# A planned four-layer trunk: pricing each change of the TensorE array's shape by kind, with new unit durations, a fixed SBUF layout and a new table of priorities

## The chip, the cores and the metric

The kernel runs on one core of one Trainium2 chip. The metric is the device time in microseconds of one execution: the median of three runs. Beside them stands one profiled execution with its trace.

## What is computed

The reference is a trunk of four residual layers, x of shape (1, 256, 1024) in float32. Layer i takes token mixer i mod 3, and every layer is followed by a SwiGLU block:

```python
for i in range(DEPTH):                       # DEPTH 4
    kind, j = i % N_MIXERS, i // N_MIXERS    # N_MIXERS 3
    h = rms_norm(x, norm_mix[i])
    if kind == 0: ...                        # RWKV-7 time mixing
...
def swiglu(h, w_gu, w_down):                 # D_FF 2816
    g, u = jnp.split(h @ w_gu, 2, axis=-1)
    return (jax.nn.silu(g) * u) @ w_down
...
def step(state, inp):                        # in rwkv7_time_mix, 256 steps, 16 heads x 64
    r_t, w_t, k_t, v_t, kk_t, a_t = inp
    sa = jnp.einsum('bhvk,bhk->bhv', state, kk_t)
    state = (state * w_t[:, :, None, :]
             - sa[..., None] * (kk_t * a_t)[:, :, None, :]
             + v_t[..., None] * k_t[:, :, None, :])
    return state, jnp.einsum('bhvk,bhk->bhv', state, r_t)
```

Layer 0 and layer 3 are RWKV-7, layer 1 is stick-breaking attention (`log_sigmoid` of the scores with a reversed cumulative sum over earlier keys), layer 2 is sparse attention over the 64 keys that an indexer of 8 heads picks for each query. Each mixer has input projections of 1024 x 1024 and an output projection; RWKV also has low-rank ("lora") projections for its decay, gate and rates.

## The kernel before, in words

**Layout of the work.** The activations lie transposed in SBUF, features on the 128 partitions in 8 chunks (`NC`), 256 tokens along the free dimension. Weights come from HBM as pieces of 128 x 1024 float32 (`raw`, 4 slots). A piece is split in two fp32r parts: a cast makes the high part `wh` (on ScalarE or VectorE), a subtraction on VectorE makes the low part `wl`; activations are split in the same way (`kx`, `gx`, `prx`, `h`, `prhl` and others). A product of 128 output features, `gemm1`, then takes for each chunk one matmul of wh with both parts of x (512 columns) and one of wl with the high part (256 columns).

**Stages.** The four layers and their SwiGLU blocks follow each other. An RWKV layer (`rwkv`, L1092) has a head (token shift `pre`, mixed inputs `xm`, their split halves, the first projections), the lora products, the rates and decays, then for chunks of 64 tokens the blocks of a triangular system. Their 32 x 32 diagonal parts are inverted on VectorE in 31 dependent steps (a multiplication into `blocks`, an addition into `inv`) with a stream transpose ahead of it and behind it. Four copies or so then move the result into `XT`; `combine` makes one more stream transpose (`xd`) for each of four pairs of head chunks, and two groups of 32 x 32 matmuls (`cmb1`, `cmb2`) complete the inverse. The recurrence over four chunks (`Chain.step`) then runs as four chains of small matmuls: pS (state by PR), Y from PR, xu (XT by u0), qu (the state's update), Y from SB. Beside all this stand the gate `pg` (a product with weights) and the bonus term, in which VectorE multiplies a sum `bn` by `vf` into `pr`, with `prs` and its halves `prhl` as steps.

**What sets the order.** Nothing is emitted directly. The kernel's code calls `Queue` objects, and `record` (L347) keeps each instruction as an `Op` with a cost from `_cost` (L263). Several matmuls may be put into one op with `unit` (L325), which may be given a duration in ns in place of the sum of its parts. An operation called on `any` has alternatives on two engines, for instance a cast on ScalarE or VectorE. `schedule` (L723) runs sixteen rounds of list scheduling over five engines (`_schedule`, L471), each with ranks from the order of the round before (`_place`), and one more round after `_nudge` has added random offsets to ranks: each row of the table `NUDGES` is a seed, a range of operations and a width. The plan with the earliest planned end is kept. `emit` (L766) then takes the SBUF slots in order of first use, those of a size that is a multiple of 128 first, and writes the instructions in planned order; each engine works through its own in that order. All instructions recorded by the plan therefore carry one line of the program, L788.

**The array's shape.** In the trace a matmul's form stands as rows by columns of the array: 128*128, 64*64, 128*64, 32*32 and so on. The planner knows only a flag, `op.parts`: either side spans at most 64 partitions. When the flag differs from that of TensorE's last operation, `_schedule` adds `SWITCH` = 95 ns to the operation's cost, and `choose` holds the operation back for another one with the same flag, unless that one's rank lies more than `STICK` = 1000 below. Where TensorE would be idle for long, `keep_warm` puts in pairs of bf16 matmuls without use (`warm_o`, L1893).

Of the kernel before, what the change touches and what calls it, by code (L numbers as in the profile page):

```python
# [14 lines left out]
F32R = mybir.dt.float32r  # L15
# [45 lines left out]


# [118 lines left out]
class Op:  # L181


    def __init__(self, eng):
        self.eng, self.instrs, self.cost, self.table, self.cols = eng, [], 0.0, None, 0.0
        self.preds, self.succs, self.alts, self.warmer, self.parts = set(), [], {}, False, False
        self.end, self.bufs, self.ns, self.lag, self.lands = 0.0, [], 0.0, 0.0, False
        self.banks = []


class Queue:
# [63 lines left out]
SWITCH = 95.0  # L255

STICK = 1000.0
# [51 lines left out]
class Plan:  # L309
# [37 lines left out]
    def record(self, eng, method, args, kw):  # L347
# [19 lines left out]
        if eng == "tensor":  # L367
            op.cols += _columns(method, outs[0], ins)
            op.parts = outs[0].p1 - outs[0].p0 <= 64 or ins[0].p1 - ins[0].p0 <= 64
# [101 lines left out]
    def _schedule(self, counts, reserve):  # L471
        engines = ("tensor", "vector", "scalar", "gpsimd", "sync")
        ready, pending, free = ({e: v() for e in engines} for v in (list, list, float))
        out, recent, parts = [], collections.deque(), False
# [68 lines left out]
        def keep_warm(t, until):  # L543

            nonlocal parts, hot
# [14 lines left out]
            t, parts = t + (SWITCH if parts else 0.0), False  # L560
# [25 lines left out]
        def choose(e, t):  # L586
# [3 lines left out]
            while ready[e] and got is None:  # L590
# [17 lines left out]
                if watch and o.parts != parts and held is None and not o.alts:  # L608
# [3 lines left out]
                if held and (o.parts != parts or o.rank < held[0][2].rank - STICK):  # L612
# [20 lines left out]
        while done < len(self.ops):  # L633
# [39 lines left out]
            if e == "tensor":  # L673
                if filled(t) < 0.8 * BUSY:
                    cost *= 2
                if o.parts != parts:
                    parts, cost = o.parts, cost + SWITCH
# [88 lines left out]
    def emit(self, nc, counts, warmer):  # L766
# [12 lines left out]
        for k in sorted(first, key=lambda k: size[k] % 128 > 0):  # L779
            first[k].get()  # L780
# [11 lines left out]
def trunk(ctx: ExitStack, tc: tile.TileContext, xT_in, vecs_in, wts, lora_in, consts_in, id32_in, nqk_in, outT, order, layers=None):  # L792
# [299 lines left out]
    def rwkv(j, layer, after):  # L1092
# [119 lines left out]
        for p in range(0, NC, 2):  # L1212
            pw = bank("lw"), bank("la")
            with unit(2, 960.0):
# [106 lines left out]
        for p in range(NC):  # L1321
            o = bank("sc"), bank("sc")
            with unit(2):
# [734 lines left out]
```

## Time and profile before

| what | value |
|---|---|
| runs | 1368.5 us median of 3 (1368.15 to 1368.95) |
| profiled execution | 1368.04 us |
| its span, first to last instruction | 1366.2 us, 25568 instructions |
| mean granted clock of TensorE | 1.000 |
| ScalarE's largest group | 350 casts `wh<-raw`, 1050 ns each |
| VectorE's largest group | 383 subtractions `wl<-raw,wh`, 1221 ns each |
| TensorE's largest group | 704 matmuls `gate<-xg,wh`, 392 ns each |
| read from HBM | 217.36 MB, in 401 pieces of 512 KB and a few more |
| busy share of the DMA queue's engines | 50.2% |

The span is the time between the first and the last instruction; the profiled execution is 1.8 us longer. PE is TensorE, DVE is VectorE, ACT is ScalarE; PEld stands for weight loads, which run beside the matmuls. Durations of matmuls overlap, so the time that one takes is read from start to start. The busy shares of all engines are shown in the prediction.

### The profile page before, as it was taken

To read this page: it belongs to the slowest core of one execution; us is meant where nothing else is said; L and a number is where in the kernel's file an instruction comes from. 1 tells how busy PE (TensorE), PEld (TensorE's weight loads), DVE (VectorE), ACT (ScalarE), POOL (GpSimd) and SP (SyncE) were. 2 spreads that over 40 slices of the span, in tenths; PEclk is the share of its full clock that TensorE was granted. 3 is DMA by queue.
4 is the path that set the end of the run, shared out by engine and by line. 5 is a ranking of instruction groups with operands and counts; after the bars stand their busy time and mean duration, and the time that the engine had idled before them with its cause. 6 is when DMAs were issued, how large, how long until landed. Compare 5 with 4: busy or idle time off the path is not lost.

```text
span 1366.2 us, 25568 instructions
## 1 busy us (share of the span) xinstructions
PE 1357.6 (99%) x10202; PEld 1189.5 (87%) x10202; DVE 1124.7 (82%) x1954; ACT 796.0 (58%) x1342; POOL 12.2 (1%) x18
## 2 busy tenths in 40 slices
PE   9999999999999999999999999999999999999998
PEld 8988898888888898888887798888899888988887
DVE  8999689886677788886679998887599996888864
ACT  7966755454455765544455965554388366665542
POOL 0100000000000000000000000000000000000000
PEclk9999999999999999999999999999999999999999
DMA  6423156555655345655654445556544231656553
GB/s 243 149 84 119 44 175 198 187 187 180 193 175 153 126 151 186 191 194 196 210 183 139 163 137 187 185 187 198 185 123 130 77 108 51 184 184 188 187 190 116
DMA packets 61335, 220.07 MB, mean 161 GB/s; under 512 B 6816, under 2 KB 8352, under 8 KB 60960
## 3 DMA queue, kind: packets, MB, share of 16 engines
q1 hardware_dynamic: 61216, 218.44, 50.2%
q8 instruction: 80, 1.31, 0.4%
q14 instruction: 39, 0.32, 0.1%
HBM read 217.36 MB, written 1.05 MB: 160 GB/s over the span
## 4 chain that ended last, share of the span: by engine, by line
PE 92%; DVE 6%; DMA 1%; issue 1%; ACT 0%; SPq 0%; DVEq 0%; ACTq 0%
PE dn L788 18%; PE gate L788 18%; PE up L788 18%; PE po L788 7%; PE qk L788 3%; PE vps L788 3%; PE rp L788 3%; PE kp L788 2%; PE z L788 2%; PE vp L788 2%; PE q L788 2%; PE k L788 2%; PE Y L788 1%; DVE blocks L788 1%; PE sc L788 1%; PE attn_o L788 1%
## 5 line engine op out<-in xcount | busy, mean ns | idle before, releaser
L788 ACT CAST wh<-raw 128x1024 fp32r<-128x1024 f32 x350 | 366.3, 1050 | 343.7 <-PE dn L788 110.1
L788 DVE TENSOR_TENSOR wl<-raw,wh 128x1024 fp32r<-128x1024 f32 x383 | 461.6, 1221 | 76.8 <-ACT wh L788 69.6
L788 PE MATMUL gate<-xg,wh 128*128 128x512 f32 x704 | 263.4, 392 | 0.0
L788 PE MATMUL up<-xg,wh 128*128 128x512 f32 x704 | 262.7, 392 | 0.0
L788 PE MATMUL dn<-h,wh 128*128 128x512 f32 (+1 forms) x720 | 246.3, 389 | 0.0
L788 PE MATMUL dn<-h,wl 128*128 128x256 f32 x704 | 197.2, 280 | 0.0
L788 PE MATMUL gate<-xg,wl 128*128 128x256 f32 x704 | 197.1, 280 | 0.0
L788 PE MATMUL up<-xg,wl 128*128 128x256 f32 x704 | 197.1, 280 | 0.0
L788 PEld LDWEIGHTS dn<-h,wh 128*128 128x128 f32 x720 | 134.0, 188 | 30.0
L788 PEld LDWEIGHTS up<-xg,wh 128*128 128x128 f32 x704 | 131.7, 187 | 28.8
L788 PEld LDWEIGHTS gate<-xg,wh 128*128 128x128 f32 x704 | 131.7, 187 | 28.6
L788 PEld LDWEIGHTS gate<-xg,wl 128*128 128x128 f32 x704 | 133.0, 189 | 0.1
L788 PEld LDWEIGHTS up<-xg,wl 128*128 128x128 f32 x704 | 133.1, 189 | 0.1
L788 PEld LDWEIGHTS dn<-h,wl 128*128 128x128 f32 x704 | 132.8, 189 | 0.0
L788 ACT CAST h<-gus 128x512 fp32r<-128x512 f32 x43 | 26.7, 621 | 53.0 <-DVE gus L788 52.9
L788 PE MATMUL vp<-xv,raw 128*128 128x256 f32 x256 | 57.3, 382 | 0.3 <-PE qct L788 0.3
L788 DVE TENSOR_TENSOR gus<-gus,rstd 128x512 f32<-128x512 f32 x88 | 57.2, 684 | 0.2
L788 PEld LDWEIGHTS vp<-xv,raw 128*128 128x128 f32 x256 | 48.0, 190 | 7.7 <-issue 0.7
L788 DVE TENSOR_TENSOR h<-gus,h 128x512 fp32r<-128x512 f32 x44 | 30.4, 691 | 24.8 <-ACT h L788 24.8
L788 PE MATMUL rp<-prx,wh 128*128 128x256 f32 x256 | 49.7, 295 | 0.0
L788 PE MATMUL kp<-kx,wh 128*128 128x256 f32 x256 | 48.4, 288 | 0.5 <-DVE kx L788 0.4
L788 PE MATMUL po<-yhl,wh 128*128 128x256 f32 x256 | 48.3, 289 | 0.0
(331 smaller groups left out, 2432.2 us busy)
## 6 DMA issues: line engine op xcount, KB each, us to landing
raw<-in_wts_dram SPq DMA_DIRECT2D x401, 512.0 KB, 3.9
lora<-in_lora_dram SPq DMA_DIRECT2D x2, 1280.0 KB, 9.7
xt<-in_xT_dram SPq DMA_DIRECT2D x4, 256.0 KB, 4.0
lora<-in_lora_dram SPq DMA_DIRECT2D x2, 512.0 KB, 5.3
inv<-in_id_dram SPq DMA_DIRECT2D x2, 512.0 KB, 3.6
out_dram<-xt SPq DMA_DIRECT2D x8, 128.0 KB, 2.9
sbt<-in_consts_dram SPq DMA_DIRECT2D x1, 512.0 KB, 3.9
consts<-in_consts_dram SPq DMA_DIRECT2D x1, 288.0 KB, 5.8
```

Source lines behind the costliest of these rows:

```text
L788: getattr(getattr(nc, o.eng), method)(*map(real, args), **{k: real(a) for k, a in kw.items()})
```

## The change

It has four parts, all of them in the planner or in the numbers that it works with.

1. *The array's shape by kind.* `op.parts` gives way to `op.shape`, the shape of the operation's first and last matmul in quarters of the array (1, 2 or 4 by 1, 2 or 4), and `op.enter`, a price by the shape that is entered. A change costs `SWITCH` (now 97) and `enter`; `choose` holds back an operation of any other shape and not only one with another flag. The planner starts in the full shape `WHOLE`, and warming matmuls bring it back there.
2. *Unit durations* become smaller where the old ones held such a change, or are given for the first time.
3. *A fixed SBUF layout.* `emit` takes the slots in the order of a list of names, `LAYOUT`, within the two groups of sizes.
4. *A new table of priorities*, 56 rows in place of 63.

```diff
+LAYOUT = (
+    "ones xt0 chmask xt1 xt2 xt3 sqa_0 QC_0 sq_0 s0_0 raw_0 s1_0 t_0 s6_0 raw_1 raw_2 t_1 t_2 t_3 raw_3 wh_0 wl_0 wh_1 wh_2 "
...
-        self.preds, self.succs, self.alts, self.warmer, self.parts = set(), [], {}, False, False
+        self.preds, self.succs, self.alts, self.warmer, self.shape, self.enter = set(), [], {}, False, [], 0.0
...
 NUDGES = [[
-    (461406, 4825, 4945, 1000), (222252, 5820, 5870, 3000), (292571, 81, 131, 1000), (91922, 1777, 1897, 1000),
...
+    (886415, 620, 640, 8000), (374831, 1759, 2059, 1000), (804050, 3305, 3605, 300), (41355, 3292, 3592, 300),
...
-SWITCH = 95.0
+SWITCH = 97.0
+WHOLE = (4, 4)
+ENTER = {(2, 4): 100.0, (1, 4): 100.0, (4, 2): 48.0, (2, 2): 48.0, (1, 1): 18.0, (4, 1): 18.0}
...
-            op.parts = outs[0].p1 - outs[0].p0 <= 64 or ins[0].p1 - ins[0].p0 <= 64
+            shape = tuple(-(-(v.p1 - v.p0) // 32) for v in (ins[0], outs[0]))
+            shape = tuple(n if n < 3 else 4 for n in shape)
+            if not op.shape:
+                op.enter = ENTER.get(shape, 100.0 if ins[0].dtype == F32R else 0.0)
+            op.shape = [(op.shape or [shape])[0], shape]
...
-                if watch and o.parts != parts and held is None and not o.alts:
+                if watch and o.shape[0] != shape and held is None and not o.alts:
...
-                if held and (o.parts != parts or o.rank < held[0][2].rank - STICK):
+                if held and (o.shape[0] != shape or o.rank < held[0][2].rank - STICK):
...
-                if o.parts != parts:
-                    parts, cost = o.parts, cost + SWITCH
+                if o.shape[0] != shape:
+                    cost += SWITCH + o.enter
+                shape = o.shape[1]
...
-        for k in sorted(first, key=lambda k: size[k] % 128 > 0):
+        def place(k):
+            n = k if isinstance(k, str) else k.name
+            return size[k] % 128 > 0, LAYOUT.index(n) if n in LAYOUT else len(LAYOUT)
+
+        for k in sorted(first, key=place):
             first[k].get()
```

The unit durations in ns, before and now: lw and la 960 to 860; sc from the sum of its parts to 900; qct 560 to 460; vtok 990 to 934; bv 980 to 934; cmb1 and cmb2 540 to 512; pS, Y, xu and qu 280 to 232; pv from the sum of its parts to 628; z of the stick-breaking layer 1000 to 976; idx 740 to 655; z of the sparse layer 1000 to 1098.

What is computed, and the matmuls that do it, stay the same; the order on each engine and the choice of the engine for operations with alternatives come out anew. Three places show it.

TensorE, in the recurrence of the first RWKV layer, behind the fourth group of 32 x 32 matmuls in the order before (pS, Y<-PR and xu are of the form 64*64, qu and Y<-SB of the form 128*64; x4 counts the matmuls of one group):

```order
L788 MATMUL cmb1_1824<-xd_1671,SB_1088 32x32 x16
L788 MATMUL pS_1845<-Sn_1814,PR_824 64x64 x4
L788 MATMUL Y_1852<-SB_1018,UV_1275 64x64 x4
L788 MATMUL qu_1859<-UV_1275,QC_857 64x64 x4
L788 MATMUL xu_1865<-u0_1857,XT_913 64x64 x4
L788 MATMUL Y_1764<-SB_1018,UV_1275 64x64 x4
L788 MATMUL Y_1852<-PR_824,Sn_1814 64x64 x4
```

and the same stretch in the new order (where the line of recorded instructions is L803):

```order
L803 MATMUL cmb1_1728<-xd_1636,SB_1087 32x32 x16
L803 MATMUL qu_1748<-UV_1355,QC_715 64x64 x4
L803 MATMUL qu_1754<-UV_1355,QC_715 64x64 x4
L803 MATMUL Y_1761<-SB_1022,UV_1355 64x64 x4
L803 MATMUL Y_1767<-SB_1022,UV_1355 64x64 x4
L803 MATMUL pS_1779<-Sn_1759,PR_821 64x64 x4
L803 MATMUL Y_1761<-PR_821,Sn_1759 64x64 x4
L803 MATMUL pS_1795<-Sn_1772,PR_821 64x64 x4
L803 MATMUL xu_1802<-u0_1793,XT_914 64x64 x4
L803 MATMUL Y_1767<-PR_821,Sn_1772 64x64 x4
```

Before, the six groups behind cmb1 take up a shape five times; now two groups of qu and two of Y<-SB stand together, then five groups of 64*64, and the nine take up a shape twice.

VectorE, at the end of the first RWKV layer's inverse, up to the transpose xd that opens `combine`, before (prhl is the split of the bonus term, vf are the layer's values):

```order
L788 TENSOR_TENSOR inv_1001<-inv_1001,blocks_1083 128x2x30
L788 CAST prhl_1476<-prs_1449 128x512
L788 TENSOR_TENSOR blocks_1083<-inv_1001 128x31
L788 TENSOR_TENSOR pr_1133<-bn_1416,vf1_114 128x512
L788 TENSOR_TENSOR inv_1001<-inv_1001,blocks_1083 128x31
L788 TENSOR_TENSOR prhl_1500<-prs_1449,prhl_1476 128x512
L788 STREAM_TRANSPOSE blocks_1083<-inv_1001 128x1024
L788 TENSOR_TENSOR pr_1133<-bn_1421,vf0_113 128x512
L788 COPY XT_913<-blocks_1083 32x16x32 x3
L788 COPY XT_925<-blocks_1083 32x16x32
L788 STREAM_TRANSPOSE xd_1569<-XT_913 128x512
```

and now:

```order
L803 TENSOR_TENSOR inv_981<-inv_981,blocks_1074 128x2x30
L803 TENSOR_TENSOR wl24_1447<-raw24_1258,wh24_1334 128x1024
L803 TENSOR_TENSOR blocks_1074<-inv_981 128x31
L803 TENSOR_TENSOR inv_981<-inv_981,blocks_1074 128x31
L803 STREAM_TRANSPOSE blocks_1074<-inv_981 128x1024
L803 COPY XT_914<-blocks_1074 32x16x32 x4
L803 CAST prhl_1531<-prs_1467 128x512
L803 STREAM_TRANSPOSE xd_1537<-XT_914 128x512
L803 TENSOR_TENSOR prhl_1558<-prs_1467,prhl_1531 128x512
L803 TENSOR_TENSOR pr_1133<-bn_1513,vf2_116 128x512
```

Of the two products with vf between the last steps of the inverse and xd, one has gone ahead and one behind (vf1, which is further down the new order); one subtraction of prhl has gone behind xd, and a wl has come among the last steps. The four copies of XT now stand together.

VectorE, at the same place of the last RWKV layer, before:

```order
L788 TENSOR_TENSOR blocks_11400<-inv_11297 128x31
L788 TENSOR_TENSOR wl325_11826<-raw325_11633,wh325_11658 128x1024
L788 TENSOR_TENSOR inv_11297<-inv_11297,blocks_11400 128x31
L788 TENSOR_TENSOR wy_11643<-raw326_11620,wy_11643 32x1024
L788 STREAM_TRANSPOSE blocks_11400<-inv_11297 128x1024
L788 TENSOR_TENSOR pr_11469<-bn_11847,vf0_113 128x512
L788 COPY XT_11242<-blocks_11400 32x16x32 x3
L788 TENSOR_TENSOR prhl_11930<-prs_11894,prhl_11920 128x512
L788 TENSOR_TENSOR pr_11469<-bn_11898,vf1_114 128x512
L788 STREAM_TRANSPOSE xd_11941<-XT_11242 128x512
L788 STREAM_TRANSPOSE xd_11951<-XT_11242 128x512
```

and now:

```order
L803 TENSOR_TENSOR pr_11388<-bn_11825,vf0_113 128x512
L803 TENSOR_TENSOR inv_11301<-inv_11301,blocks_11424 128x31
L803 COPY QC_11240<-bv_11839 128x8x64
L803 STREAM_TRANSPOSE blocks_11424<-inv_11301 128x1024
L803 TENSOR_TENSOR prhl_11911<-prs_11837,prhl_11880 128x512
L803 COPY XT_11252<-blocks_11424 32x16x32
L803 TENSOR_SCALAR prs_11909<-pr_11388,vecs_127 128x256
L803 COPY XT_11252<-blocks_11424 32x16x32 x2
L803 COPY QC_11240<-bv_11892 128x8x64
L803 STREAM_TRANSPOSE xd_11947<-XT_11252 128x512
L803 TENSOR_TENSOR prhl_11957<-prs_11909,prhl_11939 128x512
L803 TENSOR_TENSOR pr_11388<-bn_11834,vf1_114 128x512
```

Two copies from bv into QC, which ScalarE made before, stand among VectorE's rows ahead of the first xd; of the two products with vf ahead of it one has gone behind.

At the head of the first layer, VectorE's subtraction wl of the second weight piece moves from behind the first of the kx splits to behind the second. Some operations with alternatives change sides: of eight casts into prx VectorE keeps one and not four, of sixteen scalings into am it takes eight and not four, of eight copies from bv into QC two and not none, and ScalarE takes the rest of each.

More of the change, by code (lines that the diff above doesn't have):

```diff
@@ L60 @@
 CSPLIT = [0, COFF["ntri"][0], COFF["dupi"][0], NCONST]
+LAYOUT = (
+    "ones xt0 chmask xt1 xt2 xt3 sqa_0 QC_0 sq_0 s0_0 raw_0 s1_0 t_0 s6_0 raw_1 raw_2 t_1 t_2 t_3 raw_3 wh_0 wl_0 wh_1 wh_2 "
+    "wh_3 t2_0 xm_0 t2_1 xm_1 PR_0 xm_2 consts0 wl_1 xm_3 identb bonesr t2_2 wl_2 t_4 t2_3 wl_3 s7_0 xb_0 SZ_0 t2_4 dc_0 vf0 "
+    "vf1 vf3 vf2 t_5 t_6 t_7 kc0_0 kc1_0 kc2_0 eps_rms SA_0 lim eps_gn vecs omka kks_0").split()
 class Region:
@@ L473, in _schedule @@
         ready, pending, free = ({e: v() for e in engines} for v in (list, list, float))
-        out, recent, parts = [], collections.deque(), False
+        out, recent, shape = [], collections.deque(), WHOLE
         slots = {g: {k: 0.0 for k in range(counts[g])} for g in self.grouped}
@@ L543, in keep_warm @@
         def keep_warm(t, until):
-            nonlocal parts, hot
+            nonlocal shape, hot
             clear = [k for k, b in banks.items() if not b["left"]]
@@ L559, in keep_warm @@
             w, t = Op("tensor"), max(t, at)
-            t, parts = t + (SWITCH if parts else 0.0), False
+            t, shape = t + (SWITCH if shape != WHOLE else 0.0), WHOLE
             w.start, w.idx, w.warmer, hot = t, -1, (k, k != hot), k
@@ L1213, in rwkv @@
             pw = bank("lw"), bank("la")
-            with unit(2, 960.0):
+            with unit(2, 860.0):
                 for q in range(2):
@@ L1322, in rwkv @@
             o = bank("sc"), bank("sc")
-            with unit(2):
+            with unit(2, 900.0):
                 for c in range(NCH):
@@ L1399, in rwkv @@
             o = bank("qct"), bank("qct")
-            with unit(2, 560.0):
+            with unit(2, 460.0):
                 for q in range(2):
@@ L1412, in rwkv @@
             o = bank("vtok")
-            with unit(1, 990.0):
+            with unit(1, 934.0):
                 for q in range(2):
@@ L1421, in rwkv @@
             o = bank("bv")
-            with unit(1, 980.0):
+            with unit(1, 934.0):
                 for q in range(2):
@@ L1457, in combine @@
             z, zs, z2 = bank("cmb1"), t1("zs"), bank("cmb2")
-            with unit(1, 540.0):
+            with unit(1, 512.0):
                 for c in range(2 * NCH):
@@ L1465, in combine @@
                 anye.copy(zs[hi:hi + 32], z[hi:hi + 32, :S])
-            with unit(1, 540.0):
+            with unit(1, 512.0):
                 for c in range(2 * NCH):
@@ L1488, in step @@
                     u0 = t1("u0")[:, :2 * C].rearrange("p (a b) -> p a b", a=2)
-                    with unit(1, 280.0):
+                    with unit(1, 232.0):
                         for q in range(2):
@@ L1494, in step @@
                     dve.tensor_tensor(u0, ab(a[:, :2 * C]), BV[:, p0:p0 + 2, c], op=ALU.add)
-                    with unit(1, 280.0):
+                    with unit(1, 232.0):
                         for q in range(2):
@@ L1501, in step @@
                 a = bank("xu")
-                with unit(1, 280.0):
+                with unit(1, 232.0):
                     for q in range(2):
@@ L1511, in step @@
                     Sn = t1("Sn")[:, :2 * C].rearrange("p (a b) -> p a b", a=2)
-                    with unit(1, 280.0):
+                    with unit(1, 232.0):
                         for q in range(2):
@@ L1525, in step @@
                     self.Sp = Sn
-                with unit(1, 280.0):
+                with unit(1, 232.0):
                     for q in range(2):
@@ L1603, in pv @@
     def pv(o, v, vcol, ats):
-        with unit(2):
+        with unit(2, 628.0):
             for tb in range(2):
@@ L1638, in stick @@
             zs = bank("z"), bank("z")
-            with unit(1, 1000.0):
+            with unit(1, 976.0):
                 for tb in range(2):
@@ L1790, in dsa @@
                 os = bank("idx"), bank("idx")
-                with unit(2, 740.0):
+                with unit(2, 655.0):
                     for tb in range(2):
@@ L1827, in dsa @@
             pts, zs = [], (bank("z"), bank("z"))
-            with unit(1, 1000.0):
+            with unit(1, 1098.0):
                 for tb in range(2):
```

28 rows, old and new, of the table NUDGES are left out of this document.

## The prediction

> **What bounds the kernel now.** I read the page first (busy time, clock), then the waits of TensorE, then the windows of busy time, then the timeline at the places that these name. The page's lines:
>
> ```profile
> span 1366.2 us, 25568 instructions
> PE 1357.6 (99%) x10202; PEld 1189.5 (87%) x10202; DVE 1124.7 (82%) x1954; ACT 796.0 (58%) x1342; POOL 12.2 (1%) x18
> PEclk9999999999999999999999999999999999999999
> ```
>
> TensorE (PE) is busy for 1357.6 of 1366.2 us at the full clock, so only 8.6 us of the span hold no matmul at all. The view of who waited for whom, kept to TensorE, says how little of that are waits (total, times, longest in us):
>
> ```profile
> PE warm_o L1893 <- DVE eps_gn L788: 1.2, 1, 1.2
> PE bv L788 <- DVE inv L788: 0.5, 1, 0.5
> PE lora_in L788 <- DVE lora L788: 0.5, 1, 0.5
> PE cmb L788 <- DVE xd L788: 0.4, 1, 0.4
> PE kp L788 <- DVE kx L788: 0.4, 1, 0.4
> PE g L788 <- ACT EF L788: 0.3, 1, 0.3
> PE cmb L788 <- DVE pr L788: 0.3, 1, 0.3
> PE vp L788 <- PE qct L788: 0.3, 1, 0.3
> PE bn L788 <- DVE prhl L788: 0.2, 1, 0.2
> PE bv L788 <- issue: 0.2, 1, 0.2
> ```
>
> They sum to 4.3 us, 1.2 of it the start, which the change does not touch. So 3.1 us of waits can be won by a better order, and everything else must come out of TensorE's own work. All ten lie in the two RWKV layers. The windows of busy time (window, its length, then PE, PEld, DVE, ACT busy) show why: in each of these layers, up to the inverse of the 32-row blocks, VectorE (DVE) has almost no room.
>
> ```profile
> 20.00:124.00 104.00, 103.15 (x978) 94.31 (x980) 101.55 (x194) 76.02 (x137) 6.46 (x5) 1.00 0.41 132
> 124.00:187.00 63.00, 62.34 (x1103) 54.99 (x1099) 49.14 (x103) 46.16 (x108) 0.00 (x0) 1.00 0.26 78
> 993.00:1116.00 123.00, 122.41 (x1131) 109.24 (x1130) 119.36 (x226) 84.48 (x160) 3.52 (x4) 1.00 0.38 114
> 1116.00:1176.00 60.00, 59.40 (x1029) 51.49 (x1028) 46.59 (x101) 43.03 (x103) 0.00 (x0) 1.00 0.26 78
> ```
>
> VectorE stands for 2.4 of 104 us in the first layer and 3.6 of 123 in the last. There both engines bound the kernel; elsewhere TensorE alone does.
>
> **The change, part 1: what a change of shape costs.** The planner is to know it by kind; the chip charges it already. Four matmuls of one kind in the recurrence, on the timeline (start, length, form of array, count):
>
> ```profile
> 1129.05 0.45 PE L788 MATMUL qu<-UV,QC 128*64 128x64 f32 x8
> 1129.33 0.40 PE L788 MATMUL Y<-SB,UV 128*64 128x64 f32 x8
> 1129.66 0.45 PE L788 MATMUL pS<-Sn,PR 64*64 64x64 f32 x8
> 1129.95 0.40 PE L788 MATMUL Y<-PR,Sn 64*64 64x64 f32 x8
> 1130.18 0.32 PE L788 MATMUL pS<-Sn,PR 64*64 64x64 f32 x4
> ```
>
> Start to start: Y<-PR,Sn stands between two of its own shape and takes 0.23 us. qu enters 128*64 and takes 0.28; Y<-SB,UV is the last before another shape and takes 0.33; pS enters 64*64 and takes 0.29. So leaving a shape costs 0.10 us and entering one of these two 0.05 more. Entering fp32r after a small shape costs 0.10, here as the first pair of wh takes 0.34 us and not 0.24:
>
> ```profile
> 126.58 0.40 PE L788 MATMUL pg<-gx,wh 128*128 128x256 f32 x2
> 126.82 0.28 PE L788 MATMUL pg<-gx,wl 128*128 128x256 f32 x1
> ...
> 128.11 0.69 PE L788 MATMUL cmb<-xd,SB 32*32 32x32 f32 x32 [0.41 <-DVE xd L788]
> 128.73 0.50 PE L788 MATMUL pg<-gx,wh 128*128 128x256 f32 x2
> 129.07 0.27 PE L788 MATMUL pg<-gx,wl 128*128 128x256 f32 x1
> ```
>
> A warming matmul costs 0.11: six and one change out of 128*128 take 0.76 us (0.76 - 0.10 = 0.66, by 6).
>
> ```profile
> 137.07 0.83 PE L1893 MATMUL warm_o<-warm_x 128*128 128x256 bf16 x6
> 137.83 0.45 PE L788 MATMUL pS<-Sn,PR 64*64 64x64 f32 x8
> ```
>
> Counted over TensorE's whole order with the forms of the trace, shape changes go from 218 to 210: 8 x 0.10 = -0.8 us. Entries into 64*64 go from 54 to 45 and into 128*64 from 47 to 37: 19 x 0.05 = -0.95. Against it: entries into fp32r from a small shape 31 to 34 and into plain fp32 on the whole array 13 to 15, 5 x 0.10 = +0.5; into 32*32 12 to 15, between nothing and 0.05 each, taken as +0.05. Warming matmuls go from 60 to 64, +0.45. The turn from fp32 to fp32r on the whole array, which the planner still does not charge, is 9 times more; first and last matmul together show no more than 0.01 us for it. Sum: -0.75, say **-0.8 us** of TensorE's work, all on the path. By layers, counted the same way: first RWKV -1.0, stick-breaking -0.5, sparse attention and the feed-forward blocks round it +0.3, last RWKV with its feed-forward +0.4.
>
> [...]
>
> The other edits cost nothing on the chip. Unit durations and SWITCH are numbers of the planner. The fixed SBUF layout moves nothing: all 69 slots of the built program have the address and size that they have before.
>
> **Part 2: the waits.** At the head, TensorE waited for the second kx, because VectorE made a wl between the first and the second:
>
> ```profile
> 17.71 1.22 DVE L788 TENSOR_TENSOR wl<-raw,wh 128x1024 fp32r<-128x1024 f32 x1
> 18.84 0.69 DVE L788 TENSOR_TENSOR pre<-xn,rstd 128x512 f32<-128x512 f32 x1
> 19.44 0.42 DVE L788 TENSOR_TENSOR kx<-xm,kx 128x256 fp32r<-128x256 f32 x1
> ```
>
> In the new order that wl (1.13 us, start to start) comes behind, so this kx ends near 18.7 and not 19.8; the wait of 0.4 goes. Behind the moved wl stand the third kx, now near 20.5, and the matmuls of the next weight piece, which TensorE reaches near 20.7: late next, but in time by 0.2.
>
> That gain is not added to the next one, since both end at the same gate: the first cmb of the layer, which waits for xd (0.41 in the row of 128.11 above). xd stands at the end of VectorE's full stretch:
>
> ```profile
> 120.11 0.42 DVE L788 CAST prhl<-prs 128x512 fp32r<-128x512 f32 x1
> 120.44 0.21 DVE L788 TENSOR_TENSOR blocks<-inv 128x60 f32<-128x60 f32 x1
> ...
> 122.50 0.68 DVE L788 TENSOR_TENSOR prhl<-prs,prhl 128x512 fp32r<-128x512 f32 x1
> 123.11 1.23 DVE L788 STREAM_TRANSPOSE blocks<-inv 128x1024 f32<-128x1024 f32 x1
> ...
> 127.34 0.71 DVE L788 STREAM_TRANSPOSE xd<-XT 128x512 f32<-128x512 f32 x1
> ```
>
> Ahead of it now stand three casts fewer of prx (128x512, like the prhl cast: 0.33 each, -1.0; ScalarE takes them, which has 28 of these 104 us free), and one prhl pair and one product with vf are moved behind it (0.33 + 0.61 + 0.60, -1.5); smaller swaps give back 0.5. So xd is ready 2.0 us sooner, near 126.1. TensorE has 1.6 us less work ahead of that cmb and loses the head's wait, so it arrives no later than xd. Behind the cmb it has 0.6 more (of the layer's -1.0, -1.6 stand ahead). The layer ends 2.0 - 0.6 = 1.4 us sooner: 0.4 more than its work alone.
>
> In the last layer the same path is longer. From the last addition of the feed-forward block, VectorE has 0.8 us more ahead of the first xd (+2.9 and -2.1, the largest two copies of QC and two am that ScalarE had). Before, xd was just in time: two of them took from 1115.88, so the first ended near 1116.5,
>
> ```profile
> 1115.88 1.30 DVE L788 STREAM_TRANSPOSE xd<-XT 128x512 f32<-128x512 f32 x2
> ```
>
> and the cmb began 0.2 us after:
>
> ```profile
> 1116.79 0.88 PE L788 MATMUL cmb<-xd,SB 32*32 32x32 f32 x44
> ```
>
> TensorE's work ahead of it is the same in both, so 0.8 - 0.2 = +0.6 us of new wait; its bounds are nothing, if VectorE's 3.6 us of standing shrink, and 0.8 and as much again.
>
> **The sum.** -0.8 (work) - 0.4 (first layer) + 0.6 (last layer) = -0.6 us. The profiled execution took 1368.04 us (span 1366.2 and 1.8 around it), 0.5 below the median of 1368.5; 1367.4 on its scale is **1367.9** on the median's. 0.2% of the time, 2.7 us, is about what a measurement of this kernel can tell from no change.
>
> **Rivals.** *The waits go altogether.* The planner's durations are nearer to the trace's, so its plan may hold all over. For: 3.1 us of waits and nothing else in the way. Against: the plan's waits come from VectorE and ScalarE, whose prices the change leaves alone. All gone gives -0.8 - 3.1 = -3.9, 1364.6; it counts as faster only if over 1.9 of the 3.1 go.
>
> *VectorE makes the last layer late.* Its path to the inverse runs in order, and the subtractions that need a cast from ScalarE stand in it; if it waits once more there for as long as it stands in that layer now (3.6 us), every wl behind the waiting instruction and the cmb on TensorE come that much later: -0.6 + 3.6 = +3.0, 1371.5. It decides from 3.4 us of added standing. For: 97% busy there, and more work ahead of xd. Against: ScalarE is free for 38 of those 123 us.
>
> *The change does nothing that can be seen.* Fewer changes of shape only move TensorE's arrival at xd and at the DMA of the next weights; the 0.8 is given back as wait: 1368.5.
>
> **How the numbers follow.** My sum has 0.40, the change that does nothing 0.21, the waits gone 0.22, VectorE late 0.17. The first two lie within 0.2%: 0.61. The third is faster, the fourth slower. For the range, the sum's bounds are -0.8 - 0.4 - 0.6 and -0.4 + 0.8 + 0.8, so 1366.7 to 1369.7; to leave out no more than two in ten it reaches to the middle of the third case and to most of the fourth: 1364.4 to 1371.4.
>
> **What would show it.** In the profile after: 64 warm_o; four matmuls of the recurrence still at 0.23, with 0.10 and 0.05 at the changes; no wait of kp for kx at the head; the first cmb of the first layer near 126.1 and not 128.1; a wait of some 0.6 us for xd in the last layer; waits of TensorE without the start's 1.2 between 2 and 4 us. I am wrong in the count if shape changes cost another price in another neighbourhood; wrong in the waits if TensorE's list has a wait over 1 us, or one in a feed-forward block, where it has none now.

## The result and the profile after

The changed kernel takes 1377.05 us (median of six runs, 1375.15 to 1383.71), the kernel before 1368.71 beside it; the ratio is 1.0066, with a 95% interval of 1.0046 to 1.0087. It became slower by 8.3 us where 0.6 us less was forecast. The profiled execution is the longest of the six, 1383.71 us. Its page (span; busy time and share by engine; the granted clock in 40 slices):

```profile
span 1381.9 us, 25570 instructions
PE 1369.6 (99%) x10206; PEld 1196.8 (87%) x10206; DVE 1127.2 (82%) x1951; ACT 797.3 (58%) x1344; POOL 11.4 (1%) x19
PEclk9999999999999999999999999999999979999999
```

TensorE is busy 12.0 us longer than before, at almost the same number of matmuls, and one slice shows a clock of 0.7. The list of what TensorE waited for (total, times, longest in us):

```profile
PE cmb L803 <- DVE xd L803: 1.8, 1, 1.8
PE pg L803 <- DVE QC L803: 1.4, 1, 1.4
PE lora_in L803 <- DVE lora L803: 1.4, 2, 0.9
PE warm_o L1908 <- DVE eps_gn L803: 1.2, 1, 1.2
PE ss L803 <- DVE sq L803: 1.0, 1, 1.0
PE vp L803 <- PE qct L803: 0.7, 1, 0.7
PE vb L803 <- ACT ysq L803: 0.2, 1, 0.2
PE cmb L803 <- PE warm_o L1908: 0.2, 1, 0.2
```

The list is shorter than before and its longest entries are much longer: 7.9 us in all, where it was 4.3 with nothing over 0.5 behind the start. The two longest stand where an RWKV layer goes from its inverse to the recurrence, and behind both the clock falls, 0.9 and 2.2 us after the wait's end. The windows (length, busy PE, PEld, DVE, ACT, POOL, granted clock, DMA) show how far:

```profile
127.40:128.40 1.00, 1.00 (x34) 0.96 (x28) 1.00 (x3) 0.69 (x2) 0.00 (x0) 0.70 0.08 16
128.40:130.90 2.50, 2.50 (x24) 2.19 (x22) 2.44 (x5) 0.62 (x2) 0.00 (x0) 0.50 0.00 0
130.90:131.90 1.00, 1.00 (x15) 0.86 (x15) 0.97 (x3) 0.02 (x1) 0.00 (x0) 0.84 0.00 0
1123.80:1124.80 1.00, 1.00 (x26) 0.83 (x20) 1.00 (x3) 0.94 (x3) 0.00 (x0) 0.85 0.08 16
1124.80:1141.00 16.20, 16.20 (x239) 13.22 (x239) 9.68 (x17) 8.64 (x23) 0.00 (x0) 0.50 0.30 95
1141.00:1142.00 1.00, 1.00 (x26) 0.62 (x24) 0.29 (x1) 0.20 (x1) 0.00 (x0) 0.72 0.23 82
```

A clock of 0.70 over 1 us is 0.6 us at half and 0.4 at full. Counted so, the first layer spends 0.6 + 2.5 + 0.32 = 3.4 us at half the clock, the last 0.3 + 16.2 + 0.56 = 17.1, five times as long. On the timeline the two waits, and behind the second the warming matmuls: at half the clock four of them take 1.01 us to the next row, at the full clock two take 0.33 (each with a change of shape at the end; at 0.11 each and 0.10 for the change the four would take 0.54):

```profile
123.99 1.15 PE L803 MATMUL bv<-UV,SB 64*64 64x64 f32 x32
126.94 0.69 PE L803 MATMUL cmb<-xd,SB 32*32 32x32 f32 x32 [1.81 <-DVE xd L803]
...
1122.33 0.50 PE L803 MATMUL pg<-gx,wh 128*128 128x256 f32 x2 [1.43 <-DVE QC L803]
...
1130.81 1.08 PE L1908 MATMUL warm_o<-warm_x 128*128 128x256 bf16 x4
1131.82 1.07 PE L803 MATMUL cmb<-XT,zs 32*32 32x32 f32 x32
...
1144.46 0.39 PE L1908 MATMUL warm_o<-warm_x 128*128 128x256 bf16 x2
1144.79 0.45 PE L803 MATMUL qu<-UV,QC 128*64 128x64 f32 x8
```

In windows of 0.1 to 0.2 us the clock is 1.00 or 0.50, and something between only where a window holds the change: 0.50 from 127.81 for 3.41 us and from 1124.50 for 17.07 us = 5 x 3.41, and 1.00 around both. Here waits of 1.8 and 1.4 us were followed by it, and the experiments below put a number on that.

The clock is not all. By blocks, from the first matmul of each to the first of the next (us, profiled executions; where the first groups of a block stand among the last of the one before, counted from behind those; h2 is an experiment below, whose profiled execution lost nothing to the clock):

| block | before | after | h2 |
|---|---|---|---|
| RWKV, layer 0 | 186.39 | 189.03 | 186.81 |
| feed-forward | 184.26 | 186.69 | 184.79 |
| stick-breaking | 117.05 | 116.41 | 116.41 |
| feed-forward | 184.27 | 185.32 | 185.32 |
| sparse attention | 135.59 | 134.58 | 134.58 |
| feed-forward | 184.49 | 184.55 | 184.55 |
| RWKV, layer 3 | 183.65 | 193.72 | 187.51 |
| feed-forward, to the end | 185.46 | 186.59 | 184.57 |

The first feed-forward block lost 2.4 us and the last 1.1 with no wait in either and at a clock of 1.00. TensorE's matmuls that read xg (gate and up; length, busy time, count, clock, DMA share, GB/s) in 88 us of the first and of the last block, before:

```profile
212.00:300.00 88.00, 88.00 (x510) 1.00 0.59 191
1211.00:1299.00 88.00, 88.00 (x509) 1.00 0.60 191
```

and after:

```profile
212.00:300.00 88.00, 88.00 (x500) 1.00 0.58 186
1211.00:1299.00 88.00, 88.00 (x500) 1.00 0.58 184
```

In the same time 500 matmuls go through where it was 509 or 510. Start to start, a pair of wh and wl takes 346.7 ns in one and 353.3 in the other (means over some 300 pairs behind the last ss of a block); in the longer rhythm three pairs of 361, 349 and 350 ns follow each other again and again. The middle two blocks have 346.7 in both kernels.

### The profile page after: what moved, and what is told of

Read it like the earlier page. It is cut to its first block, busy times and chain, and to the rows that moved or that the text cites. A ratio compares the mean times of both kernels' runs of the same rounds, so it can differ in the third digit from the quotient of the medians.

```text
span 1381.9 us, 25570 instructions
## 1 busy us (share of the span) xinstructions
PE 1369.6 (99%) x10206; PEld 1196.8 (87%) x10206; DVE 1127.2 (82%) x1951; ACT 797.3 (58%) x1344; POOL 11.4 (1%) x19
## 3 DMA queue, kind: packets, MB, share of 16 engines
HBM read 217.36 MB, written 1.05 MB: 158 GB/s over the span
## 4 chain that ended last, share of the span: by engine, by line
PE 88%; DVE 9%; ACT 1%; issue 1%; DMA 0%; SPq 0%; DVEq 0%
PE dn L803 18%; PE gate L803 18%; PE up L803 18%; PE po L803 7%; PE kp L803 3%; PE qk L803 3%; PE vps L803 3%; PE z L803 2%; DVE blocks L803 2%; PE rp L803 2%; DVE inv L803 2%; PE q L803 2%; PE k L803 2%; DVE SB L803 1%; PE Y L803 1%; PE attn_o L803 1%
## 5 line engine op out<-in xcount | busy, mean ns | idle before, releaser
L803 ACT CAST wh<-raw 128x1024 fp32r<-128x1024 f32 x348 | 363.9, 1050 | 327.1 <-issue 99.2
L803 DVE TENSOR_TENSOR wl<-raw,wh 128x1024 fp32r<-128x1024 f32 x383 | 461.0, 1220 | 91.8 <-ACT wh L803 83.4
L803 PE MATMUL gate<-xg,wh 128*128 128x512 f32 x704 | 265.8, 396 | 0.0
L803 PE MATMUL up<-xg,wh 128*128 128x512 f32 x704 | 264.4, 395 | 0.0
L803 PE MATMUL dn<-h,wh 128*128 128x512 f32 (+1 forms) x720 | 246.7, 390 | 0.0
L803 PE MATMUL gate<-xg,wl 128*128 128x256 f32 x704 | 197.4, 280 | 0.0
L803 PE MATMUL up<-xg,wl 128*128 128x256 f32 x704 | 197.4, 280 | 0.0
L803 PE MATMUL dn<-h,wl 128*128 128x256 f32 x704 | 197.2, 280 | 0.0
L803 PEld LDWEIGHTS dn<-h,wh 128*128 128x128 f32 x720 | 134.1, 188 | 30.5
L803 PEld LDWEIGHTS up<-xg,wh 128*128 128x128 f32 x704 | 131.9, 187 | 30.8
L803 PEld LDWEIGHTS gate<-xg,wh 128*128 128x128 f32 x704 | 132.0, 187 | 30.5
L803 PEld LDWEIGHTS gate<-xg,wl 128*128 128x128 f32 x704 | 133.0, 189 | 0.2
L803 PEld LDWEIGHTS up<-xg,wl 128*128 128x128 f32 x704 | 133.0, 189 | 0.0
L803 PEld LDWEIGHTS dn<-h,wl 128*128 128x128 f32 x704 | 132.7, 189 | 0.0
L803 PE MATMUL vp<-xv,raw 128*128 128x256 f32 x256 | 56.9, 381 | 0.7 <-PE qct L803 0.7
L803 DVE TENSOR_TENSOR gus<-gus,rstd 128x512 f32<-128x512 f32 x88 | 57.0, 682 | 0.2
L803 PEld LDWEIGHTS vp<-xv,raw 128*128 128x128 f32 x256 | 48.1, 190 | 7.8 <-PE qct L803 0.8
L803 ACT CAST h<-gus 128x512 fp32r<-128x512 f32 x41 | 25.4, 620 | 50.5 <-DVE gus L803 50.3
L803 DVE TENSOR_TENSOR h<-gus,h 128x512 fp32r<-128x512 f32 x44 | 30.4, 691 | 26.2 <-ACT h L803 26.2
L803 PE MATMUL rp<-prx,wh 128*128 128x256 f32 x256 | 50.4, 297 | 0.0
L803 PE MATMUL po<-yhl,wh 128*128 128x256 f32 x256 | 49.8, 294 | 0.0
L803 PE MATMUL kp<-kx,wh 128*128 128x256 f32 x256 | 49.0, 290 | 0.1
```

The costliest lines, as they stand in the source:

```text
L803: getattr(getattr(nc, o.eng), method)(*map(real, args), **{k: real(a) for k, a in kw.items()})
```

## Experiments

After the trace I had three candidates for the 8.3 us: the longer waits themselves; the clock, lost because TensorE stands idle for long at a stretch (**idleness**) or because the small matmuls of this stretch fill little of the array (**density**); and what happens in the two feed-forward blocks. And a question above them: is it the new prices that make a worse plan, or the new table? In all runs but the last three of the table the plan of before or of after is kept as it is, and only a few operations in its finished list are changed, so that nothing else moves. The clock is the mean granted clock of an execution, lowest to highest.

| run | what | median, range (us) | ratio to before, 95% interval | clock |
|---|---|---|---|---|
| after | the change | 1377.05, 1375.15 to 1383.71 | 1.0066, 1.0046 to 1.0087 | 0.992 to 0.999 |
| e1_fill | after, two waits filled | 1376.01, 1375.26 to 1377.46 | 1.0057, 1.0045 to 1.0069 | 0.999 to 1.000 |
| e3_late1 | before, one copy more | 1369.30, 1368.76 to 1370.28 | 1.0006, 0.9997 to 1.0014 | 0.999 to 1.000 |
| h4_late2 | before, two copies more | 1370.16, 1369.70 to 1376.03 | 1.0022, 1.0012 to 1.0033 | 0.995 to 1.000 |
| e2_late3 | before, three copies more | 1372.95, 1370.12 to 1379.54 | 1.0044, 1.0025 to 1.0063 | 0.991 to 1.000 |
| h3_late3_fill | e2, its wait filled | 1370.78, 1369.56 to 1371.57 | 1.0015, 1.0007 to 1.0024 | 0.999 to 1.000 |
| g1_ss_one | e1, ss moved by one pair | 1374.07, 1373.59 to 1375.30 | 1.0044, 1.0029 to 1.0059 | 0.998 to 1.000 |
| g2_ss_two | e1, ss moved by two pairs | 1374.23, 1373.92 to 1374.66 | 1.0044, 1.0029 to 1.0059 | 1.000 |
| h1_both | e1, the better of each | 1372.33, 1371.32 to 1374.37 | 1.0029, 1.0018 to 1.0039 | 0.998 to 1.000 |
| h2_rhythm_only | after, the same moves of ss | 1371.53, 1371.11 to 1373.86 | 1.0026, 1.0017 to 1.0035 | 0.997 to 1.000 |
| k1_qc_to_act | h2, QC copied by ScalarE | 1371.99, 1370.21 to 1374.62 | 1.0025, 1.0016 to 1.0034 | 0.997 to 1.000 |
| e7 | old prices, no table | 1385.73, 1384.58 to 1387.52 | 1.0127, 1.0110 to 1.0144 | 0.997 to 0.999 |
| e6 | new prices, no table | 1387.27, 1384.13 to 1391.26 | 1.0143, 1.0126 to 1.0159 | 0.995 to 1.000 |
| e5 | old prices, new table | 1389.28, 1388.21 to 1390.37 | 1.0154, 1.0138 to 1.0169 | 0.999 to 1.000 |

### Filling the waits of the changed kernel

Ahead of the operation named by its number, pairs of warming matmuls are put into the finished list, in a bank that is free there (here and below the numbers are written into the loop):

```diff
         out, size, first = self.schedule(counts), {}, {}
+        for idx, slot, pairs in [(607, 'ps_1', 6), (5520, 'ps_0', 6)]:
+            at = next(i for i, o in enumerate(out) if o.idx == idx and not o.warmer)
+            new = [Op("tensor") for _ in range(pairs)]
+            for k, w in enumerate(new):
+                w.idx, w.warmer = -1, (slot, k == 0)
+            out[at:at] = new
```

> The changed kernel, its plan kept, with six pairs of warming matmuls put on TensorE into each of its two longest waits: ahead of the first cmb of the first RWKV layer (waited 1.8 us for xd) and ahead of the third group of pg before the first cmb of the last (waited 1.4 us for QC). The array then computes twelve matmuls of 0.11 us without use in each, 1.3 us. Idleness theory (standing idle for over a microsecond costs TensorE its full clock for the stretch behind): clock 1.000 and the stretches at half clock gone in both layers, so the time falls from 1377.1 to 1371-1374, and the profiled execution, which lost 10 us to the clock, falls most. Density theory (the small matmuls of the combination and the recurrence fill too little of the array, waits or not): the clock stays at 0.998-0.999 and the time at 1377. Waits-only theory (the time is the waits and nothing else): no change, 1377, as the warming matmuls stand inside the waits.

Measured: 1376.01, and a clock of 1.000 in four executions of five. The clock came back, which speaks for idleness (though the warming matmuls also fill the array), but the time hardly moved: 1371 to 1374 was a miss. The fifth execution, the profiled one, has 0.999: it lost the clock once, at another place (below). Its profile has the same two feed-forward blocks at 353.3 ns (500 matmuls in 88 us in each), which sent me there.

### Making the kernel before wait

One VectorE copy into XT, ahead of the first xd of the last layer, is made again (the same values):

```diff
+        for idx, n in [(5367, 3)]:      # 1 in e3_late1, 2 in h4_late2
+            at = next(i for i, o in enumerate(out) if o.idx == idx and not o.warmer)
+            out[at:at] = [out[at]] * n
```

> As the run with three copies, with one copy more: TensorE waits about 0.8 us for xd in the last layer. Idleness theory, with its point between the 1.0 us that the changed kernel stood idle without loss and the 1.4 us with it: +0.6 us, 1369.3, clock 1.000. Waits-only theory: the same. If even 0.8 us costs the clock there, 1371 or more.

> The kernel before with two copies into XT more ahead of that xd, 0.6 us each: TensorE waits about 1.5 us there, as long as the changed kernel waits in its last layer (1.4). Idleness theory with its point between 0.9 and 1.4 us: some executions lose the clock, 1369.6 without and up to 1379 with it. If only a wait of 2 us and more costs the clock there: 1369.3 to 1370.3 in every execution, clock 1.000.

> The kernel before, its plan kept, with one VectorE copy into XT ahead of the first xd of the last layer made three times more (0.6 us each, the same values again): xd comes 1.8 us later, and TensorE, which waited 0.2 us there, waits about 2.0 us. Idleness theory: the clock halves behind that wait for 3 us or more, so the time rises by 1.8 and by 1.5 to 8 more: 1372 to 1379, clock below 1.000 in the window behind. Waits-only theory: +1.8, 1370.5, clock 1.000. Density theory: the same +1.8, since the matmuls are those that ran at the full clock before.

TensorE's longest wait in the three (it is that of bn for prhl, just ahead of cmb), with one copy more:

```profile
PE bn L793 <- DVE prhl L793: 1.0, 2, 0.9
```

with two:

```profile
PE bn L793 <- DVE prhl L793: 1.7, 2, 1.5
```

and with three:

```profile
PE bn L793 <- DVE prhl L793: 2.3, 2, 2.1
```

With 0.9 us all eleven executions stay between 1368.8 and 1370.3, at 0.999 and more. With 1.5 us seven of ten lie between 1369.7 and 1370.4, and three at 1374.3, 1375.0 and 1376.0 with a clock of 0.995. With 2.1 us three of seven lie between 1370.1 and 1371.4, one at 1373.0 (0.998), and three between 1377.0 and 1379.5 with 0.991 to 0.993. So a long wait costs about its own length in all of these, and in a part of the executions 2 to 9 us more. The matmuls are the same in all three, which density alone can't explain. (The profiled executions of the three are among those at 1.000, so no trace shows where the others lost it.)

The last of them once more, with its wait filled (the fill as above, eight pairs ahead of bn):

> The kernel before with three copies into XT more ahead of the first xd of the last layer, as in the run e2 (1372.95, between 1370.1 and 1379.5), and eight pairs of warming matmuls put on TensorE into the wait of 2.1 us that this made. The added matmuls compute what is not used. Idleness theory: the wait stays as long, but the clock does not fall: 1370.2 in every execution, within 1369.5 and 1371, clock 1.000. Density or lateness theory: the scatter stays, up to 1379.

Eleven executions between 1369.56 and 1371.57, three of them over the expected 1371, the lowest clock 0.999. The median, 1370.8, is 0.6 over the expected 1370.2. For this place idleness is shown: the same lateness with the array kept busy no longer has the executions at 1373 to 1379.5.

Density is not out of it, though. The profiled executions of e1, g1 and h1 (the last two are described below) have their two long waits filled. In the head of the last layer e1 has a clock of 0.81 and 0.85 in the two windows of 5 us from 1090 to 1100, and h1 0.66 in one: 3.4 us at half the clock in each. g1, with a mean clock of 0.998, takes as long for this layer. There pv and qct, matmuls on 32 and on 64 of the array's rows, run for 3.8 us with no other between, and then vp waits 0.65 us for qct. Behind the start h1 has no longer wait; this one and the window behind it in h1, then the same window in h2, which has the same rows and the same wait:

```profile
PE vp L817 <- PE qct L817: 0.6, 1, 0.6
1090.00:1095.00 5.00, 4.46 (x13) 3.65 (x14) 4.86 (x12) 4.45 (x9) 0.00 (x0) 0.66 0.02 3
...
1090.00:1095.00 5.00, 4.93 (x22) 4.21 (x23) 4.83 (x12) 3.99 (x7) 0.00 (x0) 1.00 0.01 3
```

The last layer takes 188.8 us in the three and 187.5 in g2 and h2, so the loss cost 1.3 us. In the kernel before, four vp matmuls stand between two halves of pv, half as many qct behind them, and the wait is 0.26; neither its trace nor those of its four variants lost the clock there. So a loss also came behind a wait of 0.6 to 0.7 us that follows 3.8 us of small matmuls, in three of the seven traces of this plan (not in after, with 1.00 there, nor in g2, h2 and k1). Whether the wait or the small matmuls decide it there was not tried.

### The two feed-forward blocks

In both blocks the step of 353.3 ns began or stayed where a plain fp32 matmul, the sum of squares ss, stands between the gate and up matmuls. In the finished list pairs of gate or up matmuls are drawn ahead of ss:

```diff
+        for idx, ahead in [(1027, 952), (5926, 5870)]:    # g1_ss_one
+            o = next(o for o in out if o.idx == idx and not o.warmer)
+            out.remove(o)
+            out.insert(next(i for i, q in enumerate(out) if q.idx == ahead and not q.warmer), o)
...
+        # g2_ss_two: [(1027, 952), (1008, 952), (5926, 5869), (5956, 5869)]
+        # h1_both, h2_rhythm_only: [(1027, 952), (1008, 952), (5926, 5870)]
```

> The changed kernel with its two longest waits filled by warming matmuls (as in the run that filled them), and the two sums of squares (ss) inside the first and the last feed-forward block moved by one pair of gate or up matmuls. In those two blocks the pair of wh and wl matmuls took 353.3 ns, in the others 346.7, at the same clock and on the same addresses; the step came where ss or the block's start stood. Rhythm theory (the array and its weight loads fall into one of two rhythms where a plain fp32 matmul interrupts them, and keep it to the end of the block): moving ss can flip either block to 346.7 behind it, worth up to 2.0 us in the last block and 2.0 in the first; 1372 if both flip, 1374 if one, against 1376.0. Placement theory (the slow pairs come from what else runs in those blocks, DMA or VectorE): both stay at 353.3 and the time at 1376.

> As the run with the sums of squares moved by one pair, but by two pairs. Rhythm theory: another draw for both blocks, 1372 to 1376, with each block either at 346.7 or at 353.3 behind ss and nothing between. Placement theory: both at 353.3, 1376.

The same windows of the matmuls that read xg, with ss moved by one pair:

```profile
212.00:300.00 88.00, 88.00 (x500) 1.00 0.58 190
1211.00:1299.00 88.00, 88.00 (x510) 1.00 0.59 191
```

and by two:

```profile
212.00:300.00 88.00, 88.00 (x510) 1.00 0.60 192
1211.00:1299.00 88.00, 88.00 (x501) 1.00 0.59 186
```

Each move turned one block and left the other: 1374.07 and 1374.23, 1.9 and 1.8 us under 1376.01. The DMA share lies between 0.58 and 0.60 in all four. The two moves that worked, together:

> The changed kernel with its two longest waits filled by warming matmuls, and in the first feed-forward block the move of ss that brought its pairs to 346.7 ns behind ss (run g2), in the last one the move that brought them there (run g1). Rhythm theory: the two gains add, 2.0 and 1.8 from 1376.0: 1372.2, with all four blocks at 346.7 behind ss. If the rhythm is a matter of chance in each execution and not of the place of ss: one of the blocks is back at 353.3 and the time between 1374 and 1376.

1372.33, as the sum of the two gains has it. And without the fill:

> The changed kernel with the same two moves of ss and nothing put into its waits. Idleness and rhythm theory together: 1377.1 less 3.8 for the rhythm: 1373.2, with a clock of 0.992 to 0.999 and more scatter than the run that fills the waits too. If the clock costs nothing by itself: the same time as that run, 1372.2, and the same scatter.

1371.53, where I had expected 1373.2; its windows:

```profile
212.00:300.00 88.00, 88.00 (x510) 1.00 0.59 192
1211.00:1299.00 88.00, 88.00 (x509) 1.00 0.59 189
```

So the rhythm of the two blocks is worth 3.7 us (1376.01 to 1372.33), and in these kernels the place of ss decides it. The executions of h2 lie between 1371.1 and 1373.9 at 0.997 to 1.000: at the same waits the clock was lost less often, and for shorter, than in the six of the changed kernel; why, stays open. That h1's median is 0.8 us longer is not clear of noise, since the ranges overlap, and in the traces the fill costs its own layers nothing (g2, with it, takes 186.68 and 187.51 us for the two RWKV layers, h2 186.81 and 187.51). The sparse layer, where nothing was put in, is 0.5 to 0.7 us longer in e1, g1, g2 and h1 than in h2; the traces of e1, g2 and h1 show a short wait of qi for wl there (0.1 to 0.3). What brings it about is open.

### The rest: VectorE in the last layer

h2 is still 2.9 us behind. Its waits, without loss to the clock:

```profile
PE cmb L809 <- DVE xd L809: 1.8, 1, 1.8
PE pg L809 <- DVE QC L809: 1.4, 1, 1.4
PE warm_o L1914 <- DVE eps_gn L809: 1.2, 1, 1.2
PE lora_in L809 <- DVE lora L809: 0.8, 2, 0.5
PE vp L809 <- PE qct L809: 0.6, 1, 0.6
PE xu L809 <- DVE u L809: 0.5, 1, 0.5
```

The two copies from bv into QC that the new plan put on VectorE go back to ScalarE, the second ahead of a cast there:

```diff
+        for idx, eng, ahead in [(5475, 'scalar', 0), (5480, 'scalar', 5501)]:
+            o = next(o for o in out if o.idx == idx and not o.warmer)
+            o.eng, o.instrs = eng, [o.alts[eng][0]]
+            if ahead:
+                out.remove(o)
+                out.insert(next(i for i, q in enumerate(out) if q.idx == ahead and not q.warmer), o)
```

> The changed kernel with the two moves of ss that put its feed-forward blocks into the quick rhythm (1371.5 without anything else), and with the two copies from bv into QC of the last layer given back to ScalarE, as in the kernel before; the second of them stands ahead of ScalarE's cast into prhl there. If VectorE's added work ahead of xd is what TensorE waits for in the last layer (1.4 us for QC): VectorE loses two copies of 0.6, QC is ready a microsecond sooner, the wait falls to 0.5 or less and the first cmb comes 1.1 us sooner: 1370.4, and no execution over 1372. If ScalarE is as late as VectorE there: the wait only changes its name, 1371.5.

The wait for QC is gone, with 0.5 us of another in its place:

```profile
PE cmb L817 <- DVE xd L817: 1.8, 1, 1.8
PE vp L817 <- PE qct L817: 0.6, 1, 0.6
PE cmb L817 <- ACT zs L817: 0.5, 1, 0.5
```

and the layer is 0.9 us shorter in the profiled execution (186.57 after 187.51). The median says nothing of it, 1371.99, because six of the eleven executions lost up to 4 us to the clock; the wait of 1.8 us in the first layer and the 0.6 behind qct are still there, and since the profiled execution lost nothing, no trace shows which of them it was. The five at 1.000 have a median of 1370.7, those of h2 at 1.000 (three) 1371.4. So 0.7 to 0.9 us of the 2.9 are the two copies; "no execution over 1372" was a miss.

### Prices or table

Four whole plans: the table is taken out (`NUDGES = []`) or exchanged.

> The changed kernel without its table of priorities (the sixteen rounds of the planner alone, so another plan). If the prices by kind and the unit durations make plans in which TensorE stands idle whatever the table: 1385 or more with several stretches at half clock. If the new table is what made the plan bad: 1372 or less. Both could be: a plan without a table has not been fitted to anything, so it may lie well above either kernel; its waits and its clock tell which.

> The kernel before without its table. If plans without a fitted table are alike whatever the prices: 1382 to 1392, as the new prices without a table gave (1387.3). If the new prices are worse by themselves: 1372 or less.

> The kernel before with the new table of priorities in place of its own (prices of shape changes and unit durations as before). If the new prices made the plan bad and the table is good: 1370 or less. If a table only fits the prices that it was found with: a plan that is fitted to nothing, 1380 or more, with waits of over a microsecond and a clock below 1.000, as the new prices without a table gave (1387.3).

Without a table the new prices take 1387.27 and the old ones 1385.73; their intervals overlap. The table that was made for other prices did not help, 1389.28. The old table is worth 17 us to the old prices, the new one 10 us to the new. One plan each does not rank the two sets of prices. It suggests that the 8.3 us lie in how good a plan the table found and not in charging a change of shape by its kind, but no run has the new prices with a better table, so that is not shown.

## Why the prediction was wrong

**The count of TensorE's work held where it can be told apart.** In the blocks without long waits: stick-breaking -0.64 (forecast -0.5); the sparse layer and the feed-forward blocks around it and behind layer 0, in h2, 0.53 + 1.05 - 1.01 + 0.06 = +0.63, of which 0.3 is the rhythm (48 pairs at 353.3 before the first ss), so +0.3 (forecast +0.3, though without the block behind layer 0). There are 64 warming matmuls, and the prices of the shapes are as they were. The -0.4 for this work in the upper bound of the range is shown by no run: the traces have 0.10 at a change of shape (0.33 against 0.23, before as after), by which the eight are -0.8 and the work's sum -0.75. In the trace of after, pS enters 64*64 behind 128*64 (0.28), xu stands inside (0.23) and the second pS is the last before another shape (0.33):

```profile
1147.02 0.45 PE L803 MATMUL pS<-Sn,PR 64*64 64x64 f32 x8
1147.30 0.40 PE L803 MATMUL xu<-QC,XT 64*64 64x64 f32 x8
1147.53 0.40 PE L803 MATMUL pS<-Sn,PR 64*64 64x64 f32 x8
1147.86 0.39 PE L1908 MATMUL warm_o<-warm_x 128*128 128x256 bf16 x2
```

**The first layer's waits: right gate, wrong arrival.** xd was to be ready near 126.1. In h2, whose head is like that of before (the first kp at 17.57, then 17.37), it is: the cmb begins at 126.22.

```profile
126.22 0.69 PE L809 MATMUL cmb<-xd,SB 32*32 32x32 f32 x32 [1.80 <-DVE xd L809]
```

So the start of the cmb, which is all that this part of the sum used, was right. "It arrives no later than xd" is true as well, but not enough: TensorE arrived 1.8 us too early, since three waits that I had not counted as gone went too (bv for inv 0.5, g for EF 0.3, bv 0.2). VectorE's full stretch sets the gate; what TensorE does not wait in small pieces ahead of it, it waits there in one. I never asked what one wait of 1.8 us does that several of 0.4 don't. The term of the sum that failed here is "behind the cmb it has 0.6 more": it was 2.3 (61.8 us from 126.2 to 188.0 in h2, 59.5 before). Of the 1.7 that were missing, four waits of 0.14 to 0.16 us make 0.6. The 192 matmuls of the output projection (po) take 25.3 us from start to start and not 23.8: twelve of them are followed by some other matmul and not six. Why six more breaks cost 1.5 us, when a change of shape costs 0.10 and entering fp32r behind a small shape 0.10 more, was not settled.

**The last layer: the place right, the size short.** VectorE's added copies did make TensorE wait, 1.4 us and not 0.6, and for QC (by the list; for the bank that the copy empties, as I take it), two groups of pg ahead of the cmb where I looked. 1.4 lies within the bounds that I gave, 0 to 1.6; the low end of the range did not follow from them (it takes 0.6 off in the place where the sum adds 0.6 for this layer; with the bound of 0 it would have been 1367.3 and not 1366.7). With vp and xu (0.6 and 0.5 in h2, where before had 0.3 and none in its list) the layer and its feed-forward are 3.0 us behind in h2, where +1.0 was forecast.

**Two costs had no term at all,** and they make 5.5 of the 8.9 us by which the sum missed. The clock: about 1.8 us of the median, by subtraction only (1377.05 to 1371.53 less the 3.7 of the rhythm, though h2 has the same waits), and some 8 in the profiled execution, the excess of its two RWKV layers over h2's (2.2 + 6.2) less a head that is 0.7 later there. The trace of before has a mean clock of 1.000, so no row that I read had a price for it; the warming matmuls alone say that the plan avoids something. The rhythm of the feed-forward blocks: 3.7 us. Nothing in the trace of before shows it, apart from single pairs.

So of the median's 8.3 us 3.7 are the rhythm, which two moves of ss gave back; some 1.8 are put down to the clock; and the 2.8 that are left are waits and small pieces, net of what TensorE's work gained, of which k1 shows 0.7 to 0.9 to be the copies of QC.

**The rivals.** "VectorE makes the last layer late" had the right engine, layer and sign and put the time at 1371.5. That h2 measured 1371.53 is luck: its mechanism (one more stand of 3.6 us) did not happen, TensorE's longest wait in that layer being 1.4, and of h2's 2.9 us k1 shows only 0.7 to 0.9 to come from VectorE's added copies. "Wrong in the waits if TensorE's list has a wait over 1 us" was the sentence that came true, behind both inverses.

## What to carry to other kernels

A list of waits is not a sum: with one wait of 1.5 us (h4_late2) three of ten executions had a clock of 0.995 and took 4.3 to 6.1 us more than the median of the other seven, where the kernel before, with no wait over 0.5 us behind the start, stayed at 0.999 and more in every execution. So when a change takes small waits away ahead of a gate that stays, ask how long the one wait at the gate becomes. The table of priorities found for one set of prices was worth nothing for the other here; judge the prices without it, or find it anew as long as the old one. And when a block without waits gets longer, count its matmuls in equal windows before looking for another cause.

## What the runs showed of the hardware

The clock: with TensorE idle for 0.9 us ahead of the first cmb of the last layer none of eleven executions fell under 0.999, for 1.5 us three of ten did (0.995), for 2.1 us four of seven (0.991 to 0.998; 0.999 can hold one loss of 3.4 us, as the profiled execution of e1 shows). Behind 3.8 us of matmuls on 32 and 64 rows and a wait of 0.6 to 0.7 us the clock was lost in e1 (0.81 and 0.85 over 1090 to 1100) and h1 (0.66 over 1090 to 1095) and, by its mean of 0.998 and the length of the layer, in g1; it was not in after and h2 (1.00 over 1090 to 1095), nor in g2 and k1 (1.000 over the whole execution). The losses that the windows show are 3.4 us long at half the clock (after in its first layer, e1, h1, and e6 with 0.67 over 130 to 135), and one, in the recurrence of the changed kernel, 17.1 us, five times as long.

In the gate and up matmuls a pair of 512 and 256 columns took, at a clock of 1.00, 346.7 or 353.3 ns on the mean (509 or 510, and 500 or 501 matmuls in 88 us). The longer rhythm came where such a run of pairs began (the changed kernel's first block, 45 pairs before its first ss) or where a plain fp32 matmul broke it (its last block: 346.8 ns over 48 pairs before ss, 353.3 over 300 behind it). It held for the 300 pairs and more up to the last pair of both, and the same place gave it again in e1_fill (500 matmuls in 88 us in both). At the start of the first feed-forward block it is not the order alone: in the traces of e2_late3 and e3_late1 35 pairs ran at 353.3 where those of the kernel before and of h4_late2, with the same instructions up to there, had 346.7. Whether it changes between executions of one kernel was not seen, as each has one trace. What in the array or its weight loads makes the two was not tried.
